# Taking the copied first chunk and the products of zeros out of the projections of a two-layer decoder trunk

## The chip, the core and the metric

The kernel runs on one core of a Trainium2 chip. The core has five engines that run side by side, each with its own list of instructions: TensorE (matmuls), VectorE, ScalarE, GpSimd and SyncE, which here issues nearly all DMAs. They wait for each other through semaphores. The metric is the device time of one execution in microseconds; less is better. Inputs lie in the chip's memory at the start, and the output must lie there at the end.

## What is computed

A trunk of two layers over one sequence of 256 tokens with 1024 features. Each layer has three sub-layers: a SwiGLU feed-forward block, a token mixer, and a second feed-forward block. The mixer of layer 0 is stick-breaking attention with 16 heads, that of layer 1 a Griffin block (a short convolution and a gated linear recurrence, RG-LRU) of width 1280. Each sub-layer normalizes its input, scales and shifts it by values worked out from a conditioning vector, and adds its gated result to the trunk. All is float32. Cut to what matters here:

```python
def swiglu(h, w_gu, w_down):
    g, u = jnp.split(h @ w_gu, 2, axis=-1)      # 1024 -> 2 x 2816
    return (jax.nn.silu(g) * u) @ w_down        # 2816 -> 1024
...
for layer in range(DEPTH):
    mod = (c_act @ mod_w[layer] + mod_b[layer]).reshape(B, N_SUB, 3, D_MODEL)
    h, g = sublayer_input(x, norm_g[layer, 0], mod[:, 0])
    x = x + MACARON_W * g * swiglu(h, ffn_w_gu[layer, 0], ffn_w_down[layer, 0])
    h, g = sublayer_input(x, norm_g[layer, 1], mod[:, 1])
    ...
    x = x + g * y                               # y: attention or RG-LRU block
    h, g = sublayer_input(x, norm_g[layer, 2], mod[:, 2])
    x = x + MACARON_W * g * swiglu(h, ffn_w_gu[layer, 1], ffn_w_down[layer, 1])
return rmsnorm(x, final_norm_g)
```

## The kernel before

**Products in three passes.** The products must be as exact as float32, and TensorE is used in a rounded form of it (float32r). So each operand is split in a rounded part and the rest: a weight into `wh` and `wl` (`load`, line 504; ScalarE writes `wh` at line 519, VectorE `wl` at line 522), an activation into a high and a low part. `group` (line 536, the matmul at line 548) then issues three matmuls that add up in one PSUM bank: `wh` with the high part, `wh` with the low part, `wl` with the high part. In the profile they show as two `wh` products and one `wl`, and I call them a group of three. Weights are the stationary operand (128x128), activations the moving one (128 features x 256 tokens).

**Layout.** Activations lie transposed: a chunk `hx` holds 128 of the 1024 features for all 256 tokens, so a normalized input has eight chunks, each with a high and a low tile. They come from a ring of 20 places, 320 words apart, with a pad ahead of it (`HXPAD`). The rings `wh` and `wl` have 7 places of 1024 words each. The results of an up tile go into the arena of the phase (`arenar`), which lies behind a pad of `ARPAD` words (line 487).

**Up tiles.** `up` (line 722) makes one tile of 256 results: over eight chunks `k` and two halves `g`, 8 x 2 x 3 = 48 matmuls. A feed-forward block has 22 such tiles, `f` = 0 to 21. Block 0 (layer 0, first feed-forward block) does tiles 0 to 7 together, chunk by chunk as the weights arrive, and from f=8 on goes tile by tile. The three other blocks (1 to 3 in the text), the attention and the RG-LRU block begin with `up_first` (line 737): two tiles from the input before normalization, 258 columns wide, whose results are scaled afterwards; the normalized chunks are made beside them, and from f=2 on `up` uses them.

**Down projections.** `down` (line 666) multiplies the results of the up tiles, two at a time, by the weights back to 1024 features: a block's is 22 x 8 x 3 = 528 matmuls in groups of three, the attention's and the RG-LRU block's are shorter. The last two weight tiles are taken feature by feature, so that residuals and the next input can begin (`residual`, line 689).

**The copied chunk and the products of zeros.** `other_copy` (line 660) copies the high and the low tile of chunk 0 of each normalized input to a ring of its own, `hk`, that lies behind `hx` and a pad of `HKPAD` words, one copy on ScalarE and one on VectorE (line 664). The up tiles whose `f` is in `KICKS` (line 37: 2, 3, 7, 9, 11, 15, 19), the attention's up tiles from the third on and the up tiles of the RG-LRU block take chunk 0 from `hk`, the others from `hx`; the values are the same. `kick_op` (line 731, the matmul at line 734) issues a product of zeros, 64 columns wide and bfloat16, that adds nothing to the bank; `down` puts one after its first group of three of a given weight tile: the first one in the feed-forward blocks, the second in the attention and in the RG-LRU block. So there are six copies of a chunk, 39 tiles that use one, and six products of zeros.

**Order.** The program first builds a list of operations with costs; `schedule` (line 167) is a list scheduler that gives each engine its order and each buffer its place; then the instructions are issued. TensorE's order keeps mostly to that of the program. DMAs go out on SyncE's queue in the order of the schedule, and each waits until its buffer is free; the loads for the conditioning (`rawm`, multiplied and summed on VectorE at line 580) lie between the weights' loads in that queue.

## Time and profile before

| | |
|---|---|
| median of 3 runs | 967.43 us (967.09 to 967.57) |
| the profiled execution | 973.06 us, its span 971.4 us |
| TensorE, matmuls | 8102, busy 98% of the span |
| of them 128x256 or 128x258 at line 548 | 3236 + 1618 on hx, 1664 + 832 on arenar, 234 on hk |
| VectorE, ScalarE | busy 82% and 58% |
| DMA | 251.25 MB, mean 259 GB/s over the span |
| feed-forward blocks, from first plain up tile to the end of down | block 0 about 61 to 202 us, block 1 about 333 to 501, block 2 about 518 to 685, block 3 about 792 to 960 |

A row of the groups view has the line, the engine and its operation, the output and inputs by name, the sizes and the number of instructions; after the bar the busy time in us and the mean length of one in ns; then the idle time of the engine just before them. A row of the timeline has the start in us, the length in us, and what ran; neighbours alike are merged, with their number. Matmuls overlap in it, since each lasts longer than the distance to the next: that distance, start to start, is the pitch. A row of the windows has the stretch, its length, the busy time of TensorE's matmuls and of its weight loads with the number of those that touch the stretch, the granted clock of TensorE as a share of full speed, the DMA engines' busy share and the rate in GB/s. A row of the chain in order of time has the start, the length and what the end of the kernel hung on then. A row of the waits has who waited for whom, the total in us, how often, and the longest.

### The profile page before, as it was taken

To read this page: it belongs to the slowest core of one execution; us is meant where nothing else is said; L and a number is where in the kernel's file an instruction comes from. 1 tells how busy PE (TensorE), PEld (TensorE's weight loads), DVE (VectorE), ACT (ScalarE), POOL (GpSimd) and SP (SyncE) were. 2 spreads that over 40 slices of the span, in tenths; PEclk is the share of its full clock that TensorE was granted. 3 is DMA by queue.
4 is the path that set the end of the run, shared out by engine and by line. 5 is a ranking of instruction groups with operands and counts; after the bars stand their busy time and mean duration, and the time that the engine had idled before them with its cause. 6 is when DMAs were issued, how large, how long until landed. Compare 5 with 4: busy or idle time off the path is not lost.

```text
span 971.4 us, 19751 instructions
## 1 busy us (share of the span) xinstructions
PE 951.9 (98%) x8102; PEld 938.5 (97%) x8102; DVE 797.0 (82%) x1325; ACT 562.7 (58%) x907; POOL 3.8 (0%) x16
## 2 busy tenths in 40 slices
PE   7999999999999999999999999999999999999996
PEld 5999999999999999999999999999999999999996
DVE  7899898798998999899789999844997997555443
ACT  4385444478987864454357544443879785444343
POOL 0000000000000000000000000000000000000000
PEclk9999999999999999999999999999999999999998
DMA  8999999864665489999967999955244646545421
GB/s 315 311 354 338 352 358 355 328 243 146 249 235 202 171 312 356 356 369 348 353 245 273 330 364 354 358 196 195 110 142 163 260 151 243 207 181 207 172 100 45
DMA packets 48189, 251.25 MB, mean 259 GB/s; under 512 B 5473, under 2 KB 6369, under 8 KB 28386
## 3 DMA queue, kind: packets, MB, share of 16 engines
q1 hardware_dynamic: 47378, 249.30, 69.7%
q8 instruction: 63, 1.03, 0.4%
q10 hardware_dynamic: 720, 0.69, 0.2%
q14 instruction: 28, 0.23, 0.1%
HBM read 248.92 MB, written 1.05 MB: 257 GB/s over the span
## 4 chain that ended last, share of the span: by engine, by line
PE 79%; DVE 8%; DMA 8%; ACT 3%; issue 2%; SPq 0%; DVEq 0%; ACTq 0%
PE bank L548 73%; DMA rawm<-in_modw 4%; DMA raw<-in_gu 3%; DVE wl L522 3%; PE bank L880 2%; DVE arenaf L1059 1%; DVE rawm L580 1%; PE bank L1003 1%; ACT arenaf L498 1%; ACT wh L519 1%; PE bank L565 1%; PE bank L956 1%; PE bank L981 1%; DMA x<-in_xT 1%; DVE hpre L650 0%
## 5 line engine op out<-in xcount | busy, mean ns | idle before, releaser
L548 PE MATMUL bank<-hx,wh 128*128 128x256 f32 (+1 forms) x3236 | 566.8, 279 | 5.0 <-ACT hx L498 3.4
L519 ACT ACTIVATE wh<-raw 128x1024 fp32r<-128x1024 f32 (+1 forms) x328 | 336.9, 1046 | 309.0 <-PE bank L548 208.9
L548 PEld LDWEIGHTS bank<-hx,wh 128*128 128x128 f32 x3236 | 494.7, 189 | 8.4 <-ACT hx L498 4.3
L522 DVE TENSOR_TENSOR wl<-raw,wh 128x1024 fp32r<-128x1024 f32 (+1 forms) x328 | 389.3, 1208 | 103.0 <-ACT wh L519 102.5
L548 PE MATMUL bank<-hx,wl 128*128 128x256 f32 (+1 forms) x1618 | 450.4, 278 | 0.0
L548 PEld LDWEIGHTS bank<-hx,wl 128*128 128x128 f32 x1618 | 306.6, 190 | 0.0
L548 PE MATMUL bank<-arenar,wh 128*128 128x256 f32 x1664 | 285.0, 277 | 0.0
L548 PEld LDWEIGHTS bank<-arenar,wh 128*128 128x128 f32 x1664 | 250.7, 188 | 0.1
L548 PE MATMUL bank<-arenar,wl 128*128 128x256 f32 x832 | 229.7, 276 | 0.0
L580 DVE SCALAR_TENSOR_TENSOR rawm<-rawm,cact 128x1024 f32<-128x1024 f32 x143 | 174.1, 1221 | 30.4 <-DMA rawm<-in_modw 29.7
L548 PEld LDWEIGHTS bank<-arenar,wl 128*128 128x128 f32 x832 | 156.2, 188 | 0.0
L498 ACT ACTIVATE arenar<-a 128x256 fp32r<-128x256 f32 x88 | 35.5, 405 | 8.6 <-DVE a L767 8.4
L772 DVE TENSOR_TENSOR arenar<-a,arenar 128x256 fp32r<-128x256 f32 x88 | 36.5, 419 | 0.6 <-ACT arenar L498 0.5
L767 DVE TENSOR_TENSOR a<-bank,sg 128x256 f32<-128x256 f32 x82 | 34.0, 418 | 0.5 <-ACT sg L498 0.4
L498 ACT ACTIVATE sg<-bank 128x256 f32<-128x256 f32 x82 | 29.7, 368 | 3.0 <-PE bank L548 3.0
L548 PE MATMUL bank<-hk,wh 128*128 128x256 f32 x156 | 31.2, 291 | 0.0
L498 ACT ACTIVATE hx<-x,mf 128x256 fp32r<-128x256 f32 x40 | 18.6, 500 | 20.2 <-DVE x L689 20.2
L498 ACT ACTIVATE hx<-hpre,mf 128x256 fp32r<-128x256 f32 x48 | 23.4, 500 | 10.5 <-DVE hpre L650 8.5
L689 DVE SCALAR_TENSOR_TENSOR x<-bank,mf,x 128x256 f32<-128x256 f32 x48 | 21.6, 478 | 7.8 <-PE bank L548 7.7
L548 PEld LDWEIGHTS bank<-hk,wh 128*128 128x128 f32 x156 | 24.0, 189 | 0.5
L652 DVE SCALAR_TENSOR_TENSOR hx<-hpre,mf,hx 128x256 fp32r<-128x256 f32 x48 | 22.9, 480 | 0.9 <-ACT hx L498 0.9
L880 PE MATMUL bank<-wh,hx 128*128 128x256 f32 x128 | 23.5, 281 | 0.0
(109 smaller groups left out, 541.0 us busy)
## 6 DMA issues: line engine op xcount, KB each, us to landing
raw<-in_gu SPq DMA_DIRECT2D x79, 1024.0 KB, 6.2
rawm<-in_modw SPq DMA_DIRECT2D x144, 512.0 KB, 6.8
raw<-in_wdn SPq DMA_DIRECT2D x44, 1024.0 KB, 6.6
raw<-in_win SPq DMA_DIRECT2D x10, 1024.0 KB, 4.8
raw<-in_qk SPq DMA_DIRECT2D x8, 1024.0 KB, 4.8
raw<-in_gu SPq DMA_DIRECT2D x14, 512.0 KB, 8.1
raw<-in_wout SPq DMA_DIRECT2D x5, 1024.0 KB, 5.1
raw<-in_wv SPq DMA_DIRECT2D x4, 1024.0 KB, 6.2
```

Source lines behind the costliest of these rows:

```text
L498: act.activation(o(), i(), f, **{k: (v() if callable(v) else v) for k, v in kw.items()})
L519: act.activation(h()[:, :m], raw()[:, a : a + m], AF.Copy)
L522: dve.tensor_tensor(lo()[:, :m], raw()[:, a : a + m], f32(h()[:, :m]), ALU.subtract)
L548: pe.matmul(o(b()), wc(u()), xc(v()), start=start and n == 0, stop=stop and n == len(passes) - 1, skip_group_check=True)
L565: pr.op("PE", c_mm(n, 4), lambda: pe.matmul(o(b()), wc(w()), xc(x32()), start=start, stop=stop, skip_group_check=True), [w, x32] + ([] if ...
L580: dve.scalar_tensor_tensor(raw(), raw(), 1.0, cact(), ALU.mult, ALU.mult, accum_out=m()[:, t : t + 1])
L652: V(lambda: dve.scalar_tensor_tensor(lo()[:, :T], hp(), sh()[:, c], f32(hi()[:, :T]), ALU.add, ALU.subtract), T, [hp, (sh, d), hi], [lo], ...
L689: dve.scalar_tensor_tensor(x[d](), acc.b()[:, j * T : (j + 1) * T], gate()[:, d : d + 1], x[d](), ALU.mult, ALU.add)
L767: V(lambda: dve.tensor_tensor(a(), b()[:, T:], sg(), ALU.mult), T, [(b, (1, 0)), sg], [a])
L772: V(lambda: dve.tensor_tensor(y[1](), a(), f32(y[0]()), ALU.subtract), n, [a, y[0]], [y[1]])
L880: pe.matmul(o, u()[:, tb * P : (tb + 1) * P], v()[:, c0 : c0 + 256], start=start and n == 0, stop=k == KD - 1 and n == 2, skip_group_check ...
L956: pe.matmul(zb[e]()[:, BL[i]], v()[rows, kc], w()[rows, qc], start=False, stop=i == 1 and n == 2, skip_group_check=True)
```

## The change

`other_copy`, `kick_op`, the ring `hk` with its pad, the list `KICKS` and the arguments that steered them go. All up tiles take chunk 0 from `hx`, and the down projections have no product of zeros. The ring and its pad took 528 words of each partition (16 and 2 x 256); `ARPAD` grows by 16, so that what comes after `pad1` moves by 512 words, and what lies between moves by 528.

```diff
-HXPAD, HKPAD, ARPAD = 112, 16, 184
-KICKS = (2, 3, 7, 9, 11, 15, 19)
+HXPAD, ARPAD = 112, 184 + 16
...
-    const.tile([P, HKPAD], F32, tag="pad2", name="pad2")
-    hkr, _ = ring("hk", 2, T, F32R)
...
         for d in range(KD):
             norm_chunk(gen, d, q)
-        other_copy(gen)
-
-    def other_copy(gen):
-        hi, lo = hcur[gen][0]
-        h2, l2 = hkick[gen] = Buf(hkr), Buf(hkr)
-        A(h2, lambda: f32(hi()[:, :T]), AF.Copy, T, [hi], [h2])
-        V(lambda: dve.tensor_copy(l2(), f32(lo()[:, :T])), T, [lo], [l2])
-
-    def down(l, s, nxt, srcs, ys, nlast, hook=None, post=None, n32=0, kicks=(0,)):
+
+    def down(l, s, nxt, srcs, ys, nlast, hook=None, post=None, n32=0):
...
                     for k in (2 * c, 2 * c + 1):
                         step(d, k)
-                        if d == 0 and k == 2 * c and c in kicks:
-                            kick_op(*place[d])
...
-    def up(acc, ws, gen, kick=False):
+    def up(acc, ws, gen):
...
-                h = hkick[gen] if kick and k == 0 and gen in hkick else hcur[gen][k]
...
-                      lambda u, c0=c0: u[:, c0 : c0 + P], h, lambda v: v[:, :T], T, k == KD - 1)
-
-    def kick_op(acc, j):
-
-        b = acc.b
-        pr.op("PE", 130.0, lambda: pe.matmul(b()[:, j * T : j * T + 64], zero, ident[:, :64], start=False, stop=False,
-                                             skip_group_check=True), [(b, "start")], [(b, j)])
+                      lambda u, c0=c0: u[:, c0 : c0 + P], hcur[gen][k], lambda v: v[:, :T], T, k == KD - 1)
...
-            other_copy((0, 0))
...
-            up(acc, load(gu[j, f], CH, f"gu_{j}_{f}", chained if j == 0 and f == f0 else None), (l, s), f in KICKS)
+            up(acc, load(gu[j, f], CH, f"gu_{j}_{f}", chained if j == 0 and f == f0 else None), (l, s))
```

The calls in `attention` and `rglru` lose the same argument.

More of the change, by code (lines that the diff above doesn't have):

```diff
@@ L601, in mod_final @@
             V(lambda: dve.tensor_scalar(fo(), mi(), 1.0, wt, ALU.add, ALU.mult), n, rr, ww)
-    ssq, hcur, gcur, hkick = {}, {}, {}, {}
+    ssq, hcur, gcur = {}, {}, {}
     def add_square(gen, d):
@@ L911, in q_proj @@
             acc = Acc(f"qk{f}")
-            up(acc, q_load(f), (l, s), True)
+            up(acc, q_load(f), (l, s))
             def put2(g, scale):
@@ L1038, in attention @@
         down(l, s, nxt, [wo[:, 2 * c : 2 * c + 2, :].rearrange("p k d -> p (k d)") for c in range(4)],
-             lambda k: (os_[k], slice(0, T)), 2, lambda c: hook(8 + c), tail, kicks=(1,))
+             lambda k: (os_[k], slice(0, T)), 2, lambda c: hook(8 + c), tail)
     def rglru(l, s, nxt):
@@ L1100, in xb_proj @@
                 acc = Acc(f"xb{n2}")
-                up(acc, load(win[1, n2], CH, f"xb{n2}"), (l, s), True)
+                up(acc, load(win[1, n2], CH, f"xb{n2}"), (l, s))
                 def evict(e, xb):
@@ L1110, in gate_proj @@
             acc = Acc(f"gt{n2}")
-            up(acc, load(win[0, n2], CH, f"gt{n2}"), (l, s), True)
+            up(acc, load(win[0, n2], CH, f"gt{n2}"), (l, s))
             b = acc.b
@@ L1168, in rglru @@
         down(l, s, nxt, [wout[:, 2 * c : 2 * c + 2, :].rearrange("p k d -> p (k d)") for c in range(NB)],
-             lambda k: ys[k], 2, n32=N32, kicks=(N32,))
+             lambda k: ys[k], 2, n32=N32)
     def final():
```

## The prediction

> **What bounds the kernel now.** I read the busy line of TensorE, the clock line and the chain of work that ended last on the page; then the chain in order of time; then, in short windows, the groups of matmuls by operands and the timeline of TensorE.
>
> ```profile
> PE 951.9 (98%) x8102; PEld 938.5 (97%) x8102; DVE 797.0 (82%) x1325; ACT 562.7 (58%) x907; POOL 3.8 (0%) x16
> ...
> PEclk9999999999999999999999999999999999999998
> ...
> PE 79%; DVE 8%; DMA 8%; ACT 3%; issue 2%; SPq 0%; DVEq 0%; ACTq 0%
> ```
>
> The chain is TensorE for 79% of the span. In order of time it is TensorE alone over whole feed-forward blocks (start, length, how many matmuls):
>
> ```profile
> 60.66 82.70 PE bank L548 x722
> 143.40 65.61 PE bank L548 x573
> ...
> 327.04 114.77 PE bank L548 x1008
> 443.64 7.98 DMA rawm<-in_modw
> ...
> 518.52 107.95 PE bank L548 x944
> 626.52 65.39 PE bank L548 x573
> ...
> 786.30 115.20 PE bank L548 x1011
> 901.55 56.90 PE bank L548 x501
> ```
>
> So the pitch of the matmuls (start to start) sets the time there, and nothing on the page tells the pitch. It isn't one number. These are the matmuls of 41 to 53 us, then those of 106 to 125 us, both 128x256 on the same tiles, and both windows' clock and counts:
>
> ```profile
> L548 PE MATMUL bank<-hx,wl 128*128 128x256 f32 x35 | 9.8, 281 | 0.0
> ...
> L548 PE MATMUL bank<-hx,wl 128*128 128x256 f32 x56 | 15.5, 276 | 0.0
> ...
> 41.00:53.00 12.00, 12.00 (x104) 12.00 (x104) 1.00 0.95 338
> 106.00:125.00 19.00, 19.00 (x170) 19.00 (x169) 1.00 0.92 339
> ```
>
> The granted clock is 1.00 in both, and neither idles, yet one lasts 281 ns and the other 276. The pitch itself comes from the first and last rows of the timeline of each stretch (the wl product of each group of three):
>
> ```profile
> 41.19 0.28 PE L548 MATMUL bank<-hx,wl 128*128 128x256 f32 x1
> ...
> 53.20 0.28 PE L548 MATMUL bank<-hx,wl 128*128 128x256 f32 x1
> ...
> 106.32 0.28 PE L548 MATMUL bank<-hx,wl 128*128 128x256 f32 x1
> ...
> 125.02 0.28 PE L548 MATMUL bank<-hx,wl 128*128 128x256 f32 x1
> ```
>
> Between the first pair lie 34 groups of three: 12.01 us / 102 = 117.7 ns. Between the second pair lie 55: 18.70 / 165 = 113.3 ns. I call them the slow and the fast pitch; the step is **4.4 ns a matmul**, 3.9%. Each holds for as long as nothing disturbs it, and the copied chunk is what moves the kernel from one to the other. The timeline where the first one runs:
>
> ```profile
> 71.48 0.28 PE L548 MATMUL bank<-hx,wl 128*128 128x256 f32 x1
> 71.60 0.40 PE L548 MATMUL bank<-hx,wh 128*128 128x256 f32 x2
> 71.83 0.28 PE L548 MATMUL bank<-hx,wl 128*128 128x256 f32 x1
> 71.95 0.40 PE L548 MATMUL bank<-hk,wh 128*128 128x256 f32 x2
> ...
> 73.26 0.28 PE L548 MATMUL bank<-hx,wl 128*128 128x256 f32 x1
> ...
> 73.60 0.28 PE L548 MATMUL bank<-hx,wl 128*128 128x256 f32 x1
> 73.94 0.28 PE L548 MATMUL bank<-hx,wl 128*128 128x256 f32 x1
> ```
>
> Ahead of hk a group takes 0.35 us, twelve matmuls after it began a group takes 0.34, and it stays so through f=10 to the next hk.
>
> **The change part by part.** *What it saves.* Two rows of ScalarE and VectorE go, six times each, and with them their wait; of these one VectorE copy (at 514.65) stands in the chain. An hk chunk met at the fast pitch costs a little, as the timeline of f=11 shows, and so does a product of zeros:
>
> ```profile
> PE bank L548 <- ACT hx L498: 3.4, 2, 2.6
> ...
> L664 DVE CAST hk<-hx 128x256 fp32r<-128x256 f32 x6 | 1.8, 292 | 0.1
> ...
> 104.58 0.28 PE L548 MATMUL bank<-hx,wl 128*128 128x256 f32 x1
> ...
> 105.98 0.28 PE L548 MATMUL bank<-hx,wl 128*128 128x256 f32 x1
> ...
> 143.08 0.28 PE L548 MATMUL bank<-arenar,wl 128*128 128x256 f32 x1
> 143.20 0.20 PE L734 MATMUL bank<-ident,zero 128*128 128x64 bf16 x1
> ...
> 143.91 0.28 PE L548 MATMUL bank<-arenar,wl 128*128 128x256 f32 x1
> ```
>
> From 104.58 to 105.98 are four groups: 1.40 us for 1.36, so 0.04 us; 21 of the 25 hk chunks in the feed-forward blocks meet the fast pitch (all but the first of each block): 0.85 us. From 143.08 to 143.91 are two groups and the zeros: 0.83 for 0.68, 0.15 us, six times 0.9 us. With the 0.29 us of the copy the change saves **2.0 us**. Nothing that is removed issued a DMA, no queue is moved past, and no wait is added. The buffers that follow move down by 2112 bytes, and the phase tiles by 2048; the chunks, the weights and the 256-wide products keep their place relative to each other, so I cost the move at 0, between nothing and the whole step of 4.4 ns if it counts. The planner gets fewer operations and may order some others differently; I cost that at 0 too, within 1 us either way (the longest wait of TensorE on ScalarE's hx is 2.6 us, in the first row of the fence).
>
> *What is late next.* What hk did has now to come about by itself. How the kernel enters a pitch when nothing is put in for it can be seen in three kinds of places: after a stall in the first block, in the attention's output projection, and in the wide tiles that open the other blocks. The windows are 29 to 33 us, 296.8 to 300.4 and 328 to 332:
>
> ```profile
> L548 PE MATMUL bank<-hx,wh 128*128 128x256 f32 x25 | 4.4, 276 | 0.0
> ...
> L548 PE MATMUL bank<-arenar,wl 128*128 128x256 f32 x10 | 2.8, 281 | 0.0
> ...
> L548 PE MATMUL bank<-hx,wl 128*128 128x258 f32 x12 | 3.4, 283 | 0.0
> ```
>
> And the timeline of the wide tiles, its first and last group in the last window:
>
> ```profile
> 328.20 0.28 PE L548 MATMUL bank<-hx,wl 128*128 128x258 f32 x1
> ...
> 332.16 0.28 PE L548 MATMUL bank<-hx,wl 128*128 128x258 f32 x1
> ```
>
> So the fast pitch does come unaided (29 us), the slow one also exists in a down projection (297 us: arenar, before its zeros), and the two wide tiles run at 283 ns, slower still. For f=9 of block 0 the forecast is plain: the timeline shows the slow pitch through all of f=8, over a tile's border, up to hk. For f=2 of blocks 1 to 3 the matmul before is a wide one at 283 ns, and which pitch follows is not shown. Bounds: 0 (fast at once) and 6.7 ns a matmul (the pitch of the wide tiles: 33 matmuls in 3.96 us from 328.20 to 332.16, 120.0 ns). I take 4.4, the only other pitch that plain 256-wide tiles show, and let it last into the down projection, since a border between tiles ends neither pitch.
>
> In the RG-LRU block the chain has another engine where the up tiles run:
>
> ```profile
> 708.28 1.59 DVE arenaf L1059 x4
> ...
> 736.46 6.72 ACT arenaf L498 x15
> ```
>
> *The sum.* An up tile has 8 chunks x 2 halves x 3 products = 48 matmuls, a down projection of a block 22 x 8 x 3 = 528.
> Block 0: 13 tiles (f=9 to 21) and down, 1152 x 4.4 ns = 5.1 us.
> Block 1: 20 tiles, 960 x 4.4 = 4.2 us; its down (2.3 us more) runs from 441 to 501 us, where the chain is the mod loads, not TensorE (443.64 above). TensorE then waits for those at the block's end (3.4 us on ScalarE's hx, above), so I count the down at 0; without that cover it costs its 2.3.
> Blocks 2 and 3: 1488 x 4.4 = 6.6 us each.
> Attention: six up tiles of 48 (each entered anew after other products, so half) and 192 in the output projection (half): 1.1 us.
> RG-LRU: its up tiles lie where the chain is VectorE's convolutions and ScalarE's exponentials, so 0; its output projection 192 x 4.4 = 0.8.
>
> Together 24.4 us, less 2.0: **+22.4 us**. The profiled execution took 973.06 us (span 971.4), 0.6% over the median of 967.43; on the median this gives 989.8, and I say **990 us**.
>
> *The skill against it.* The Trainium skill, page "TensorE: Matmul & The Clock Gate", section "Back-to-back issue gap", gives one gap for a width, N/2.4 + 2.5, which is 109 ns for 256 columns. Its page "SBUF — State Buffer", section "Who interferes with whom", has TensorE's two read ports independent and says that "PE and ACT never wait on anyone". By these the address of a chunk can't change a pitch, and the change would only save. The rows at 276 and 281 ns, one clock and one shape, speak against it.
>
> **The rivals.**
> *Faster: the fast pitch comes by itself.* If the first plain 256-wide matmuls after the wide tiles and after the stall near 60 us fall into the fast pitch, nothing is lost and the 2.0 us are saved: 965.4. For it: the row at 29 us, and that after hk's own uneven pitch (71.95 to 73.26) the plain chunks end in the fast one. Against it: all of f=8 at the slow pitch. It decides with the pitch of f=2 in blocks 1 to 3. The rule of the skill named above gives this result too. Chance 0.13.
> *Some blocks only.* Block 0 stays slow, which the trace nearly shows, and blocks 1 to 3 find the fast pitch (or one or two of them don't): 5.1 + 1.9 - 2.0 = +5.0, 972.4, and up to 984 with two of the other blocks at 6 each. Chance 0.28.
> *A still slower pitch.* The 120.0 ns of the wide tiles goes on into the plain ones of blocks 1 to 3: 2.2 ns more on 2880 up matmuls and two downs of 528, 8.7 us: 999. Against it: no plain tile of the trace shows 120. Chance 0.12.
> *The change doesn't do what it says*: it shifts addresses along with taking the copies away, so the pitch might move for that reason. It would show as a pitch that no tile of before has; it is within the cases above.
>
> **How the numbers follow.** Forecast 0.47, some blocks 0.28, faster 0.13, slower still 0.12. Leaving out the faster end and a part of the slowest, the range is 967 to 999. A measurement of this kernel can tell about 0.2% (1.9 us) from no change: the faster rival lies just at that edge, so I halve it, and give 0.03 of the mixed case to no change: faster 0.07, same 0.10, slower 0.83.
>
> **What would show it.** After the change: groups of hx matmuls at 281 ns and a triple of 0.35 us in windows in the middle of blocks 1, 2 and 3, and arenar at 281 in their downs, with the granted clock still 1.00; each TensorE piece of the chain longer by 3.9%; TensorE's waits no longer than before. I am wrong if blocks 1 to 3 show 276 with no hk in them, if the down projections return to 276 by themselves, or if what TensorE loses is found as waits of other engines.

## The result and the profile after

The changed kernel takes **971.75 us** (median of 10 executions, 969.84 to 980.76); the kernel before, beside it on the same chip, 967.5 (10 executions, 966.21 to 971.26). The ratio is 1.0053, 95% interval [1.0031, 1.0075]: slower, as forecast, but by 4 to 5 us and not by 22. In a second session both were run again: 968.74 (ratio 1.0003 [0.9987, 1.0019]) and 973.38 (1.0056 [1.0036, 1.0075]). Of all executions here one counts as slow, the profiled one of the kernel with copies in the mixers only (983.05 us, over 1.5% above that kernel's fastest, at the usual granted clock of 0.997), and the ratios leave it out.

The changed kernel's profiled execution took 971.68 us, its span is 970.0. Its page, the busy line, the clock and the chain's shares:

```profile
PE 949.2 (98%) x8096; PEld 935.1 (96%) x8096; DVE 794.7 (82%) x1319; ACT 561.3 (58%) x901; POOL 3.8 (0%) x16
...
PEclk9999999999999999999999999999999999999999
...
PE 72%; DMA 14%; DVE 10%; issue 3%; ACT 1%; SPq 0%; DVEq 0%; ACTq 0%
```

TensorE is busy 2.7 us less than before (951.9), and its share of the chain fell from 79% to 72%; DMA's rose from 8% to 14%. The chain in order of time, its long pieces:

```profile
61.27 51.75 PE bank L545 x454
119.59 8.25 DMA rawm<-in_modw
...
185.37 7.87 DMA rawm<-in_modw
...
327.63 98.30 PE bank L545 x864
427.86 8.44 DMA rawm<-in_modw
...
518.93 170.73 PE bank L545 x1499
...
785.31 171.75 PE bank L545 x1512
```

A long piece tells the pitch by itself: 98.30 us / 864 = 113.8 ns in block 1, 113.9 in block 2, 113.6 in block 3. Before, 114.77 / 1008 gave 113.9. There is no 3.9% in any of them. The matmul groups confirm it. The first two rows are 345 to 420 us (block 1's up tiles) and 445 to 495 (its down projection), the third is 758 to 777 us (the RG-LRU block's output projection); none of these stretches holds a copied chunk or a product of zeros:

```profile
L545 PE MATMUL bank<-hx,wl 128*128 128x256 f32 x221 | 61.0, 276 | 0.0
...
L545 PE MATMUL bank<-arenar,wl 128*128 128x256 f32 x148 | 40.8, 276 | 0.0
...
L545 PE MATMUL bank<-arenar,wl 128*128 128x256 f32 x54 | 15.2, 281 | 0.0
```

This is the sign that I had named for being wrong: 276 with no hk. All four feed-forward blocks of this execution run at the fast pitch from f=8 or f=3 to the end of the down projection. Only the RG-LRU block's output projection is slow, and half of the attention's up tiles (three of six).

So the time went elsewhere. Where the two traces part first is the stretch 40 to 80 us, at the end of the eight tiles that block 0 does together. The windows, with columns for TensorE's matmuls, its weight loads, VectorE, ScalarE, GpSimd, then the granted clock, DMA share and GB/s; first the kernel before, then the changed one:

```profile
40.00:62.00 22.00, 21.73 (x180) 21.12 (x179) 19.97 (x38) 12.74 (x17) 0.00 (x0) 1.00 0.96 346
62.00:80.00 18.00, 18.00 (x157) 18.00 (x157) 17.88 (x30) 14.80 (x28) 0.00 (x0) 1.00 0.87 334
```

```profile
40.00:62.00 22.00, 19.33 (x151) 18.06 (x152) 18.92 (x38) 11.34 (x14) 0.00 (x0) 1.00 0.93 315
62.00:80.00 18.00, 18.00 (x162) 18.00 (x161) 15.70 (x24) 14.27 (x28) 0.00 (x0) 1.00 0.82 303
```

In 40 to 62 us TensorE works 19.33 us instead of 21.73: 2.4 us of new idle time, at the same clock. These are waits for normalized chunks; in the kernel before the view of TensorE's waits is empty in this stretch:

```profile
PE bank L545 <- DVE hx L649: 1.8, 3, 0.9
PE bank L545 <- ACT hx L495: 0.7, 2, 0.4
```

The longest of them ends at 48.35 us. Here is what VectorE did just ahead of that chunk, before and then after, and the row of ScalarE, after, that it waited for:

```profile
46.22 1.22 DVE L522 TENSOR_TENSOR wl<-raw,wh 128x1024 fp32r<-128x1024 f32 x1
47.35 0.48 DVE L652 SCALAR_TENSOR_TENSOR hx<-hpre,mf,hx 128x256 fp32r<-128x256 f32 x1
```

```profile
46.67 1.23 DVE L519 TENSOR_TENSOR wl<-raw,wh 128x1024 fp32r<-128x1024 f32 x1 [1.07 <-ACT wh L516]
47.81 0.48 DVE L649 SCALAR_TENSOR_TENSOR hx<-hpre,mf,hx 128x256 fp32r<-128x256 f32 x1
...
45.58 1.06 ACT L516 ACTIVATE wh<-raw 128x1024 fp32r<-128x1024 f32 x1 [4.38 <-DMA raw<-in_gu]
```

In both a weight split stands ahead of the chunk. After, it waits 1.07 us for `wh`, since ScalarE waited 4.38 us for a weight to land (1.75 us at the same place before), and the chunk comes behind it.

From 62 to 80 TensorE is full in both, so nothing is lost there at once, but VectorE does 24 operations instead of 30 and the DMAs move 303 GB/s instead of 334. VectorE's timeline there, before and then after, shows the same pattern again:

```profile
63.46 0.42 DVE L767 TENSOR_TENSOR a<-bank,sg 128x256 f32<-128x256 f32 x1
63.80 1.22 DVE L522 TENSOR_TENSOR wl<-raw,wh 128x1024 fp32r<-128x1024 f32 x1
64.93 0.75 DVE L767 TENSOR_TENSOR a<-bank,sg 128x256 f32<-128x256 f32 x2
```

```profile
64.07 0.42 DVE L748 TENSOR_TENSOR a<-bank,sg 128x256 f32<-128x256 f32 x1
66.54 2.45 DVE L519 TENSOR_TENSOR wl<-raw,wh 128x1024 fp32r<-128x1024 f32 x2 [2.06 <-ACT wh L516]
68.90 0.42 DVE L748 TENSOR_TENSOR a<-bank,sg 128x256 f32<-128x256 f32 x1
```

Before, one weight split stands between the first and the second `a` product, and its `wh` is there. After, two splits stand there, and the first waits 2.06 us for ScalarE; the `a` products behind it wait too. ScalarE's timeline of the changed kernel has the same hole one step earlier, before a weight that has not landed:

```profile
62.83 0.38 ACT L495 ACTIVATE sg<-bank 128x256 f32<-128x256 f32 x1 [0.30 <-PE bank L545]
65.45 1.06 ACT L516 ACTIVATE wh<-raw 128x1024 fp32r<-128x1024 f32 x1 [2.23 <-DMA raw<-in_gu]
```

No operation was added there. The planner put the same operations in another order: numbered without the copies and the zeros, both kernels have the same 5080. Within block 0, 75 of VectorE's, 27 of ScalarE's and 28 of SyncE's loads lie in stretches whose order differs, and none of TensorE's; from the attention on it is 250, 164, 16, and 48 of TensorE's. On SyncE's queue the load of the parameters goes out with 14 weight loads ahead of it instead of 23, and the loads of the weights and of the conditioning change places in short stretches.

### The profile page after: what moved, and what is told of

The parts are those of the page before. It is cut to its first block, busy times and chain, and to the rows that moved or that the text cites. A ratio compares the mean times of both kernels' runs of the same rounds, so it can differ in the third digit from the quotient of the medians.

```text
span 970.0 us, 19708 instructions
## 1 busy us (share of the span) xinstructions
PE 949.2 (98%) x8096; PEld 935.1 (96%) x8096; DVE 794.7 (82%) x1319; ACT 561.3 (58%) x901; POOL 3.8 (0%) x16
## 4 chain that ended last, share of the span: by engine, by line
PE 72%; DMA 14%; DVE 10%; issue 3%; ACT 1%; SPq 0%; DVEq 0%; ACTq 0%
PE bank L545 65%; DMA rawm<-in_modw 10%; DMA raw<-in_gu 3%; DVE wl L519 3%; DVE rawm L577 2%; PE bank L860 2%; PE bank L1057 1%; PE bank L983 1%; PE bank L562 1%; DVE x L679 1%; PE bank L936 1%; DVE hx L649 1%; DVE hpre L647 1%; PE bank L961 1%; DVE hx L639 1%
## 5 line engine op out<-in xcount | busy, mean ns | idle before, releaser
L545 PE MATMUL bank<-hx,wh 128*128 128x256 f32 (+1 forms) x3392 | 592.4, 279 | 7.6 <-ACT hx L495 3.5
L545 PEld LDWEIGHTS bank<-hx,wh 128*128 128x128 f32 x3392 | 516.1, 189 | 12.8 <-DVE hx L649 5.7
L545 PE MATMUL bank<-hx,wl 128*128 128x256 f32 (+1 forms) x1696 | 470.8, 278 | 0.0
L545 PEld LDWEIGHTS bank<-hx,wl 128*128 128x128 f32 x1696 | 319.6, 188 | 0.0
L679 DVE SCALAR_TENSOR_TENSOR x<-bank,mf,x 128x256 f32<-128x256 f32 x48 | 21.6, 478 | 7.7 <-PE bank L545 7.6
L649 DVE SCALAR_TENSOR_TENSOR hx<-hpre,mf,hx 128x256 fp32r<-128x256 f32 x48 | 22.5, 477 | 1.4 <-ACT hx L495 1.4
L647 DVE SCALAR_TENSOR_TENSOR hpre<-x,mf,rst 128x256 f32<-128x256 f32 x48 | 21.9, 479 | 0.5
L495 ACT ACTIVATE arenaf<-arenaf 128x768 f32<-128x768 f32 (+1 forms) x31 | 22.0, 736 | 0.4
```

The source lines that it names most:

```text
L495: act.activation(o(), i(), f, **{k: (v() if callable(v) else v) for k, v in kw.items()})
L545: pe.matmul(o(b()), wc(u()), xc(v()), start=start and n == 0, stop=stop and n == len(passes) - 1, skip_group_check=True)
L647: V(lambda: dve.scalar_tensor_tensor(hp(), x[d](), gs()[:, c], q(), ALU.mult, ALU.mult), T, [x[d], (gs, d), q], [hp], ptr=1)
L649: V(lambda: dve.scalar_tensor_tensor(lo()[:, :T], hp(), sh()[:, c], f32(hi()[:, :T]), ALU.add, ALU.subtract), T, [hp, (sh, d), hi], [lo], ...
L679: dve.scalar_tensor_tensor(x[d](), acc.b()[:, j * T : (j + 1) * T], gate()[:, d : d + 1], x[d](), ALU.mult, ALU.add)
```

## The experiments

All ratios are to the kernel before, run beside each on the same chip. The kernels before and after, in the second session:

> The kernel before, run again with a profile of its own. Theory A (a pitch is entered anew at each stall or change of products and then held; hk makes each entry end in the fast one): about 967.5 us; blocks 0 to 3 at 276 ns from their first hk on, whatever pitch block 0 had before it. Rival B (what the change lost comes from the places that moved or from another order, not from the copies or zeros): also 967.5, so this run only gives the base and how much two profiles of one kernel differ ahead of 60 us.

> The changed kernel, run again with a profile of its own. Theory A: most runs 970 to 972 us, some 5 to 11 us longer, because block 0 (5.1 us) or block 2 (6.6 us), which begin behind a stall, enter the slow pitch by chance in some runs; if this profile is of a longer run, one of these blocks shows 281 ns through up tiles and down projection. Rival B: the longer runs show no block at 281, and the time is lost as waits.

The other ratios are to all runs of the kernel before in the same session, 17 to 33 each.

Two theories to begin with. **Pitch**: some stretches run slow without the copies, only fewer than forecast, and that is the 4 us. **Order**: the planner's other order costs them, whatever the pitch. In the recorded expectations the first is theory A; rival B is the order, at first together with the places; rival C puts the loss on the zeros, and rival D on late loads.

### Which part of the change costs: copies, zeros, places

The copies stay and the products of zeros go:

```diff
-                        if d == 0 and k == 2 * c and c in kicks:
+                        if d == 0 and k == 2 * c and c in ():
```

> The kernel before without its six products of zeros, the copied chunks kept. Theory A: the four blocks keep the fast pitch from up into down without them, so 4 x 0.15 us are saved; the RG-LRU block's output projection turns slow (0.8 us lost, as after the change) and the attention's has an uncertain 0.4: within 967 to 968.5, the same as before. Rival C (the zeros carry what the change lost): 970 to 972.

967.15 us, ratio 0.9990 [0.9974, 1.0006].

The zeros stay and the copies go, in the places of before:

```diff
-        other_copy(gen)
...
-                h = hkick[gen] if kick and k == 0 and gen in hkick else hcur[gen][k]
+                h = hcur[gen][k]
...
-            other_copy((0, 0))
```

> The kernel before with its zeros, but chunk 0 always from hx and no copies made; the two tiles stay allocated, so all places are those of before. Theory A: attention up tiles and the first RG-LRU tiles enter slow in part (1.3 us lost, less 0.85 saved), block 0 and block 2 by chance, with the down projections mended by the zeros: 968 to 970 us, single runs up to 3 or 4 us longer. Rival C (the zeros carry it all): 966.5 to 967. Rival B (places or order): as before, 967.5.

971.47 us, 1.0033 [1.0016, 1.0050]. The loss comes with the copies' removal and not with the zeros', though the time is 1.5 us above what theory A had expected at most. But this kernel also got the changed order, so the two theories stay.

The changed kernel in the places of before (the ring `hk` and its pad are kept and left empty):

```diff
-HXPAD, ARPAD = 112, 184 + 16
+HXPAD, HKPAD, ARPAD = 112, 16, 184
...
+    const.tile([P, HKPAD], F32, tag="pad2", name="pad2")
+    hkr, _ = ring("hk", 2, T, F32R)
```

> The changed kernel with the two tiles and their pad left allocated and unused, so that all places are those of before; order, copies and zeros as after the change. Theories A and B: as the changed kernel, 971 to 974 with single runs up to 980. Only if the moved places carry the loss: 967 to 968.5.

970.09 us, 1.0039 [1.0019, 1.0059]: beside the changed kernel's 1.0056 no difference that this can tell. The places that the change moved aren't the cause.

### How few copies do

All copies are made, but used only by f=8 in block 0 and f=3 in the others; the mixers as before, no zeros in the blocks:

```diff
-    def down(l, s, nxt, srcs, ys, nlast, hook=None, post=None, n32=0, kicks=(0,)):
+    def down(l, s, nxt, srcs, ys, nlast, hook=None, post=None, n32=0, kicks=()):
...
-            up(acc, load(gu[j, f], CH, f"gu_{j}_{f}", chained if j == 0 and f == f0 else None), (l, s), f in KICKS)
+            up(acc, load(gu[j, f], CH, f"gu_{j}_{f}", chained if j == 0 and f == f0 else None), (l, s), f == (8 if j == 0 else 3))
```

> The kernel before with far fewer disturbances: in the blocks one tile each takes the copied chunk (f=8 in block 0, f=3 in blocks 1 to 3) and no product of zeros; the attention and the RG-LRU block as before. Theory A (a pitch once entered is held, so one disturbance behind the last stall is enough): 21 copied chunks of 0.04 us and 4 products of 0.15 us less, so 1.2 us under before, and single runs spread no further than those of before. Rival D (the blocks up to block 2 run close to the DMA limit, so what TensorE saves there comes back as waits for late loads at the entry to the attention or to block 2): only block 3's part is left, 0.3 to 0.4 us.

**966.12 us, 0.9981 [0.9966, 0.9996]**: the lowest ratio here, though the intervals of the kernel without zeros and of the next one overlap it.

The same without any copies or zeros in the mixers:

```diff
-        other_copy(gen)
+        if gen not in ((0, 1), (1, 1)):
+            other_copy(gen)
...
-                        if d == 0 and k == 2 * c and c in kicks:
+                        if d == 0 and k == 2 * c and c in ():
...
-            up(acc, q_load(f), (l, s), True)
+            up(acc, q_load(f), (l, s))
...
-                up(acc, load(win[1, n2], CH, f"xb{n2}"), (l, s), True)
+                up(acc, load(win[1, n2], CH, f"xb{n2}"), (l, s))
...
-            up(acc, load(win[0, n2], CH, f"gt{n2}"), (l, s), True)
+            up(acc, load(win[0, n2], CH, f"gt{n2}"), (l, s))
```

> The changed kernel with the copied chunk put back in one tile of each block only (f=8 in block 0, f=3 in the others), none in the attention and the RG-LRU block, no zeros; places as before. Theory A (chance entries of blocks 0 and 2 make the longer runs of the changed kernel): the long runs are gone, all within 968.5 to 971.5, because the attention and the RG-LRU block still lose about 1.5 to 2 us. Rival D (late loads make the longer runs): 971 to 974 with single runs up to 977, as after the change.

967.35 us, 0.9985 [0.9972, 0.9998], below what both theories expected. Both kernels have the order of before in block 0. In it one use of the copy a block is enough, and the mixers need none; whether any copy is needed shows below.

The opposite: copies and zeros in the mixers only.

```diff
-        other_copy(gen)
+        if gen in ((0, 1), (1, 1)):
+            other_copy(gen)
...
-    def down(l, s, nxt, srcs, ys, nlast, hook=None, post=None, n32=0, kicks=(0,)):
+    def down(l, s, nxt, srcs, ys, nlast, hook=None, post=None, n32=0, kicks=()):
...
-            other_copy((0, 0))
...
-            up(acc, load(gu[j, f], CH, f"gu_{j}_{f}", chained if j == 0 and f == f0 else None), (l, s), f in KICKS)
+            up(acc, load(gu[j, f], CH, f"gu_{j}_{f}", chained if j == 0 and f == f0 else None), (l, s), False)
```

> The changed kernel with copied chunks and products of zeros put back in the attention and the RG-LRU block only; none in the blocks. Theory A: 1.5 to 2 us under the changed kernel, best runs at 967, but its long runs stay (block 0 or 2 entering slow: 5 and 6.6 us). Rival D: the same best runs, and long runs too, but with the blocks at 276 ns in a profile and the time in waits at the entries. If the longer runs go away here as well, both are wrong.

Eleven executions take 973.33 us (967.12 to 978.89), 1.0047 [1.0025, 1.0069], no less than the changed kernel, where 1.5 to 2 us less was expected. The profiled one took 983.05 us and shows what a block looks like that enters slow. Groups at 535 to 620 us and at 640 to 690:

```profile
L548 PE MATMUL bank<-hx,wl 128*128 128x256 f32 x242 | 68.0, 281 | 0.0
...
L548 PE MATMUL bank<-arenar,wl 128*128 128x256 f32 x143 | 40.2, 281 | 0.0
```

In the timeline block 2 has 117.78 ns from 526.7 to 696.1 us, 1438 matmuls without a break, up tiles and down projection: 6.4 us. So the slow block of the prediction exists, at about the price given there (6.6). How often it comes is counted below; three other kernels' profiles, of 973.76 to 977.03 us, show one as well.

### The pitch set by the place of the chunk

The changed kernel with the pad ahead of `hx` taken out and put behind (e5), so that the chunks, and the small buffers behind them up to the arenas, lie 448 bytes lower; weights and arenas stay:

```diff
-HXPAD, ARPAD = 112, 184 + 16
+HXPAD, ARPAD = 112, 184 + 16 + 112
...
-    const.tile([P, HXPAD], F32, tag="pad0", name="pad0")
```

> The changed kernel with the pad of 112 words ahead of the hx ring taken out and as many put into the pad ahead of the arenas, so that only the chunks move, by 448 bytes, to the kind of place the copied chunk had. Theory A with its cause in the place (the pitch depends on where the chunk lies against the weights): the plain up tiles of all blocks and mixers run at 119 to 120 ns, 3500 matmuls x 6 ns = about 21 us more, 990 to 996, the down projections fast again. If the place doesn't matter: 970 to 974.

1002.91 us, 1.0351 [1.0330, 1.0372]. Groups at 345 to 450 us (block 1's up tiles) and 460 to 500 (its down):

```profile
L544 PE MATMUL bank<-hx,wl 128*128 128x256 f32 x292 | 82.7, 283 | 0.0
...
L544 PE MATMUL bank<-arenar,wl 128*128 128x256 f32 x114 | 32.0, 281 | 0.0
```

The plain up tiles run at 120.00 ns (961 matmuls from 338.53 to 453.86 us), the wide tiles' pitch, which no plain tile of before had shown; the downs of blocks 1 to 3 at 117.78 behind them. The operations are the changed kernel's; the move alone costs 31 us, more than the 21 expected, because the down projections behind turned slow too (74 up tiles at 6.7 ns a matmul are 23.7 us, three downs at 4.4 ns 7.0). Of the buffers that moved, the chunks are the ones these tiles read; whether the others matter too wasn't tried apart. The formula that the prediction took from the Trainium skill, page "TensorE: Matmul & The Clock Gate", section "Back-to-back issue gap", goes by the width alone, and the page calls it that of an isolated matmul. The run shows that at one width and a granted clock of 0.997 the pitch in a stream depends on the place as well.

### Order against pitch

The kernel before with its whole plan (x), in which the copies and the zeros are planned and not issued. Some tiles read other values than the reference's, since the planner gives the place of chunk 0 away before they read it there:

```diff
-        h2, l2 = hkick[gen] = Buf(hkr), Buf(hkr)
-        A(h2, lambda: f32(hi()[:, :T]), AF.Copy, T, [hi], [h2])
-        V(lambda: dve.tensor_copy(l2(), f32(lo()[:, :T])), T, [lo], [l2])
+        h2, l2 = hkick[gen] = Same(hkr, hi), Same(hkr, lo)
+        pr.op("ACT", c_act(T), lambda: None, [hi], [h2])
+        V(lambda: None, T, [lo], [l2])
...
-        pr.op("PE", 130.0, lambda: pe.matmul(b()[:, j * T : j * T + 64], zero, ident[:, :64], start=False, stop=False,
-                                             skip_group_check=True), [(b, "start")], [(b, j)])
+        pr.op("PE", 130.0, lambda: None, [(b, "start")], [(b, j)])
```

> The schedule of the kernel before with nothing in the places of the copies and zeros: the planner still counts them, so all queues keep the order of before, but no copy and no product of zeros is issued and chunk 0 is read from hx. Theory A (the chance entries of blocks 0 and 2 into the slow pitch carry the loss): 971 to 974 us, single runs up to 980, as the changed kernel. Rival B (the planner, without the copies, put the mod loads later in the DMA queue of block 0, and that carries the loss): 967 to 969, since the RG-LRU block's 1.4 us are lost and about 1.5 saved; long runs only where an entry is slow.

967.90 us, 0.9994 [0.9979, 1.0009].

The changed kernel's plan with all copies and zeros issued (z), hung on to the operations ahead of them so that the planner doesn't see them:

```diff
+        if d == 0 and copied(gen):
+            also(a_op, lambda: act.activation(hkt[0], f32(hi()[:, :T]), AF.Copy))
+            also(v_op, lambda: dve.tensor_copy(hkt[1], f32(lo()[:, :T])))
...
+                            also(pr.last_pe, lambda b=place[0][0].b: pe.matmul(
+                                b()[:, :64], zero, ident[:, :64], start=False, stop=False, skip_group_check=True))
```

> The schedule of the changed kernel with all copies, copied chunks and products of zeros of the kernel before issued again inside neighbouring operations, so that the DMA queue keeps the order of the changed kernel. Theory A: 967 to 968.5 us, as before, no long runs. Rival B: 970 to 973, the loss stays though every block shows 276 ns after its first copied chunk; the time is lost up to the first plain tile, at the entry of the attention and of block 2.

973.00 us, 1.0048 [1.0033, 1.0064].

And the changed plan with copies in the blocks only, used at f=8 and f=3, without zeros; beside the last kernel:

```diff
     def copied(gen):
-        return True
+        return gen not in ((0, 1), (1, 1))
```

> The changed kernel's schedule with the copied chunk in one tile of each block only (f=8 in block 0, f=3 in the others). Theory A: 967 to 968, like the run with these same tiles in the order of before, and no long runs. Rival B: 970 to 972, because the order is that of the changed kernel, but the long runs (975 and more) are gone, since no block stays slow.

971.66 us (967.86 to 977.85), 1.0038 [1.0018, 1.0057]. I had expected the long executions to go with the copies; they stayed, and the profiled one (975.21 us) has all blocks fast and its loss in waits at the entries of the attention and of block 2.

With the kernels before and after, the first two settle the first question: **without any copy in the order of before nothing is lost; with all copies in the changed order all is lost.** On the way z shows what a copy does. Its block 2 ran slow from 520.6 us on. Groups at 522 to 543 us and at 550 to 600, and between them TensorE's timeline where the copied chunk (hk) of f=7 runs:

```profile
L548 PE MATMUL bank<-hx,wl 128*128 128x256 f32 x60 | 16.9, 281 | 0.0
...
L548 PE MATMUL bank<-hx,wl 128*128 128x256 f32 x141 | 39.0, 276 | 0.0
...
543.18 0.28 PE L548 MATMUL bank<-hx,wl 128*128 128x256 f32 x1
543.30 0.40 PE L738 MATMUL bank<-hk,wh 128*128 128x256 f32 x2
...
544.26 0.28 PE L548 MATMUL bank<-hx,wl 128*128 128x256 f32 x1
...
544.60 0.28 PE L548 MATMUL bank<-hx,wl 128*128 128x256 f32 x1
544.94 0.28 PE L548 MATMUL bank<-hx,wl 128*128 128x256 f32 x1
```

A group takes 0.35 us up to 543.18 and 0.34 from 544.26 on. The copied chunk of f=3, whose second group ran at 521.04 us, had not ended the slow pitch.

### Which part of the order

Four kernels move only loads on SyncE's queue and leave the other engines' orders. The kernel before with the parameters' load early, with the other shifts of the changed kernel, and with both; then the changed kernel with the shifts taken back. `resequenced` sorts the loads by a list of their kinds (weights, conditioning, parameters) and keeps all other queues:

```diff
-    order = pr.schedule()
+    order = resequenced(pr.schedule(), WANT)
```

> The kernel before, with all its copies and products of zeros, in which one load alone moves on SyncE's queue: that of the parameters (pars<-in_par) goes out with 14 weight loads of block 0 ahead of it, as in the changed kernel, and not with 23; the orders of the other engines stay. If this load ahead of the weights is what costs the 4 us: 971 to 973 us and a DMA rate of some 300 GB/s from 62 to 80 us of the span. If it is the shifts between weight loads and modulation loads, or the orders of ScalarE and VectorE: 967.5 to 969 us.

> The kernel before, with all its copies and products of zeros; on SyncE's queue the modulation loads and weight loads follow each other as in the changed kernel (some ten shifts by one place in blocks 0 to 2), and the load of the parameters keeps its place behind 23 weight loads. If the shifts are the cause: 971 to 973 us. If the parameters' load or the other engines' orders are: 967.5 to 969 us.

> The kernel before, with all its copies and products of zeros, and the whole order of SyncE's queue from the changed kernel; the orders of TensorE, VectorE, ScalarE and GpSimd stay as before. If the order of the loads is all of the loss: 971.5 to 974 us, as with the changed kernel's whole schedule and all copies (973.0). If the orders of ScalarE and VectorE carry it: 967.5 to 969 us.

> The changed kernel, without copies and zeros, in which the modulation and weight loads of SyncE's queue follow each other as before the change; the parameters' load stays early and the orders of TensorE, VectorE and ScalarE stay those of the changed kernel. If the shifts of modulation loads are the cause: 966 to 968.5 us. If the parameters' early load or the other engines' orders are: 970 to 972.5 us.

Called v1 to v4 here, in this order, they take 968.04 (0.9996 [0.9981, 1.0011]), **978.69** (1.0106 [1.0079, 1.0134]), **979.88** (1.0116 [1.0095, 1.0138]) and 973.65 (1.0053 [1.0032, 1.0073]). The parameters' load alone costs nothing. v2 and v3 came out far above what was expected of either cause: they lose 11.3 and 12.5 us, in another place. TensorE's waits of v3:

```profile
PE bank L1052 <- ACT arenar L547: 6.8, 1, 6.8
PE bank L597 <- ACT hx L547: 4.1, 2, 2.6
```

The 6.8 us are one wait in the attention, and v2 has it too (6.7 us). The attention lasts 127.5 and 128.4 us in them against 117.2. That these loads come in an order that the engines beside them aren't planned for is the likely reason; it wasn't tried apart. In the start, on the other hand, v3 runs as before, and v4, with the loads' shifts taken back, as changed; 40 to 62 and 62 to 80 us of v3, then of v4:

```profile
40.00:62.00 22.00, 22.00 (x188) 22.00 (x188) 20.91 (x42) 12.96 (x17) 0.00 (x0) 1.00 0.98 349
62.00:80.00 18.00, 18.00 (x158) 18.00 (x157) 17.88 (x30) 14.52 (x28) 0.00 (x0) 1.00 0.86 324
```

```profile
40.00:62.00 22.00, 19.84 (x160) 18.84 (x161) 19.38 (x39) 11.95 (x16) 0.00 (x0) 1.00 0.92 326
62.00:80.00 18.00, 18.00 (x162) 18.00 (x161) 14.87 (x23) 13.71 (x26) 0.00 (x0) 1.00 0.80 281
```

So the start's loss goes with what ScalarE and VectorE have in their queues, and the place of a load can't be tried apart from them without new waits. The last two kernels therefore move all engines together, in one part of the program only. Both are the changed kernel, without copies and zeros; the first (s1) has the operations of block 0 in the order of before, the second (s2) those from the attention on. `rearranged` puts the listed operations of each queue into the other plan's order:

```diff
-    order = pr.schedule()
+    order = rearranged(pr.ops, pr.schedule(), pr.loads)
```

> The changed kernel, without copies and products of zeros, in which the operations of block 0 stand on VectorE, ScalarE and SyncE in the order of the kernel before (75, 27 and 28 of them at another place); from the attention on all is as changed. If the loss comes from all orders together and part of it in block 0's start (1.8 us in the medians of the stages), 969 to 970.5 us, and the stretch from 62 to 80 us moves 330 to 350 GB/s again. If all of the loss begins in the start: 966 to 968. If none of it does: 971 to 972.5.

> The changed kernel, without copies and products of zeros, in which block 0 stays as changed and from the attention on the operations of TensorE, VectorE, ScalarE and SyncE stand in the order of the kernel before (48, 250, 164 and 16 of them at another place). If the loss comes from all orders together: 967.5 to 969.5 us, with the attention's entry and block 2's back at 117.2 and 180.7 us and the start's rate from 62 to 80 us still near 300 GB/s. If all of the loss begins in the start: 971 to 972.5. If none of it does: 966 to 968.

967.67 us (12 executions) and 972.93 (6). The windows of the first, then of the second:

```profile
40.00:62.00 22.00, 21.32 (x178) 20.53 (x178) 21.05 (x39) 13.70 (x19) 0.00 (x0) 1.00 0.92 341
62.00:80.00 18.00, 18.00 (x156) 18.00 (x154) 17.88 (x30) 14.12 (x26) 0.00 (x0) 1.00 0.94 362
```

```profile
40.00:62.00 22.00, 19.34 (x154) 18.06 (x153) 18.95 (x38) 11.06 (x15) 0.00 (x0) 1.00 0.93 318
62.00:80.00 18.00, 18.00 (x155) 18.00 (x154) 15.05 (x24) 13.86 (x26) 0.00 (x0) 1.00 0.84 299
```

**With block 0 in the order of before the loss is gone from most executions, and with all the rest in the order of before it is there.** The ratios are 1.0018 [0.9992, 1.0044] and 1.0052 [1.0031, 1.0073]. They overlap, because four of the first kernel's executions are long (972.1 to 979.5) while the other eight lie between 965.2 and 968.4; the second's lowest is 968.5. So these two point to block 0's start and don't settle it. The first kernel's profile is one of the long ones (973.76 us). Groups at 100 to 130 and 160 to 190 us:

```profile
L622 PE MATMUL bank<-hx,wl 128*128 128x256 f32 x86 | 24.2, 281 | 0.0
...
L622 PE MATMUL bank<-arenar,wl 128*128 128x256 f32 x85 | 23.9, 281 | 0.0
```

Block 0 came in slow and stayed so from 53.97 to 206.02 us. From the start of f=8 to its end it takes 141.33 us instead of 136.00: 5.33 us, which taken off leaves 968.4. The second kernel's profile (975.75 us) has the same slow block, so 5.33 us of it are pitch as well; the other long executions of both have no profile.

### What all twenty profiles show together

*The start.* In ten profiles block 0 has the order of before, in ten the changed one. From 40 to 62 us TensorE is busy 21.09 to 22.00 us in the first ten (median 21.6) and 19.19 to 20.01 in the others (19.65): 1.95 us lost, with no overlap. TensorE's waits for normalized chunks in this stretch are 0 to 0.9 us in the first ten and 1.6 to 2.9 in the others. From 62 to 80 us the DMAs move 319 to 375 GB/s and 275 to 304.

*The pitch.* Nine profiles are of kernels that use no copy in the blocks and leave the chunks where they lie to each other (one has before's zeros, one the mixers' copies). Of their 36 blocks four are slow up to the end of the down projection: block 0 in s1 and s2, block 2 in e7 (copies in the mixers only) and v4, each 1245 to 1438 matmuls, 5.5 to 6.4 us. So four of the nine executions have one, and blocks 1 and 3 never. Ten profiles are of kernels that use a copy in the blocks, and of their 40 blocks none is slow to its end; but block 2 of z ran slow over the copied chunk at 521.04 us, up to that at 543.30. (The twentieth is that of the kernel with the moved chunks.)

Block 0 comes to its f=8 at the slow pitch in six of the ten profiles with the order of before and in one of the other ten. So the f=8 that the prediction saw is no rarity in that order. The changed order's waits in 40 to 62 us start the stream anew more often, which may be why; no run shows it.

The stages of six of them in us, each from the trace's first matmul of the stage to that of the next (block 0 from its f=8, block 3 to the last matmul):

| | time | start to f=8 | block 0 | attention | block 1 | block 2 | RG-LRU | block 3 |
|---|---|---|---|---|---|---|---|---|
| before, second session | 968.55 | 65.8 | 136.31 | 117.18 | 181.07 | 181.07 | 93.95 | 182.58 |
| no copies, order of before (x) | 967.33 | 64.2 | 136.00 | 118.94 | 180.64 | 180.64 | 93.95 | 182.15 |
| changed | 971.68 | 66.7 | 136.00 | 118.52 | 180.67 | 181.79 | 95.21 | 182.20 |
| changed, second session | 970.71 | 65.1 | 136.00 | 117.23 | 180.67 | 183.59 | 95.22 | 182.20 |
| block 0 as before (s1) | 973.76 | 65.0 | 141.33 | 117.03 | 180.67 | 182.10 | 95.02 | 182.18 |
| the rest as before (s2) | 975.75 | 67.2 | 141.33 | 116.84 | 180.67 | 183.52 | 94.00 | 182.18 |

Over all profiles the median of the start is 64.9 us for the ten with the order of before in block 0 and 66.6 for the other ten: 1.7 us. The two ranges overlap, 63.4 to 66.3 and 65.1 to 68.0.

## Why the prediction was right in direction and wrong in size

**Right: the two pitches, and that they last.** 117.78 and 113.33 ns came back in every trace at a granted clock near 1.00, and a slow entry could go through all borders into the down projection (1438 matmuls in e7).

**Right: the price of a slow block.** 5.1 us forecast for block 0, 5.33 measured (f=8, which I had left out, is slow too); 6.6 for block 2, 6.4 measured. The RG-LRU's output projection was to lose 0.8 and lost 0.83 (188 matmuls x 4.4 ns).

**Right: the saving.** For the blocks it was 0.85 us for the copied chunks and 0.15 for each zeros: 1.45. Measured, from the table: 0.31 + 0.40 + 0.43 + 0.38 = 1.5 (row 1 against row 3, block 2 against row 2).

**Wrong: that the blocks enter slow.** This is the step that failed, "For f=9 of block 0 the forecast is plain" and, for f=2 of blocks 1 to 3, "I take 4.4, the only other pitch that plain 256-wide tiles show". In the changed kernel's two profiles all eight blocks find the fast pitch unaided, and so do 32 of 36 in the nine profiles without copies in the blocks. What I took for evidence was one profile, in which f=8 of block 0 was slow, as it often is in the order of before but not in the changed one, and which shows blocks 1 to 3 only with a copy in their first tiles. The copy isn't needed for the fast pitch; it mostly ends the slow one where that occurs. 22.5 of the 24.4 us rested on that step. The row at 29 us, quoted for the faster rival, was the better guide.

**Wrong: the order.** "The planner gets fewer operations and may order some others differently; I cost that at 0 too, within 1 us either way". It costs more than that in block 0's start alone, 1.7 to 2.0 us, and it is what made the change slower: x, z and the kernels before and after together show it, and s1 and s2 agree. So the right direction was luck: it came from the term that stood at 0, not from the blocks' pitch. In the changed kernel's profile, against row 1: +1.0 to f=8, +1.3 in the attention, +0.7 in block 2, +1.3 in the RG-LRU block (0.8 of it pitch, as forecast), and -1.1 in the other blocks, together +3.2, which is the difference of the two spans (970.0 and 966.8). How the rest beyond the start divides isn't settled: the attention's and block 2's entries differ by up to 2 us between executions, and block 2 is no shorter in s2, which has the order of before there.

**The faster rival** had 965.4 and a chance of 0.13. Its mechanism, the fast pitch by itself, came true in 32 of 36 blocks; x, which has it without the changed order, took 967.9. The rule of the Trainium skill's page "TensorE: Matmul & The Clock Gate", section "Back-to-back issue gap", gave that time too, but not for a reason that holds: more than one pitch exists at one width, and e5, in which the chunks moved, took 120.00 ns where the changed kernel took 113.33. The prediction read the formula as that of a stream, which the page doesn't say.

**The rival "some blocks only"** named 972.4, close to the 971.75. Its mechanism wasn't the one: in the changed kernel's two profiles no block is slow. Its longer executions, 974.6 to 980.8 us in the first session, have no profile; some of them may have a slow block, as four of the nine above do, so how much of its loss over many executions is pitch stays open.

**Open.** What in the start's order does it: the late weight, the weight split that waits for it in VectorE's queue and the chunk behind it are what the trace shows, but no kernel moved these alone. What makes an entry slow or fast, and what in the place of a chunk sets the pitch, wasn't found.

## What to carry to other kernels

When a list scheduler plans the kernel, taking any operation out is also a change of order everywhere behind it, so compare each engine's order of the two kernels first, and separate the two by planning operations that aren't issued. Before a step is priced at "always", count how often the trace shows it, over several profiles: a thing that repairs a state that comes only at times looks like the cause of the good one. And count it in the changed kernel's order too, where it can be rarer. And move loads together with the operations that use them: here the loads' order of one plan among the operations of the other cost 11.3 and 12.5 us.

## What the runs showed of the hardware

The same 128x256 float32r matmul has three pitches at the full granted clock, 113.33, 117.78 and 120.00 ns. Which of the first two holds could change where the stream starts anew after a stall (in z twelve matmuls up to 516.85 us run at the fast one, and those behind the wait of 0.22 us at 517.34 at the slow one, with no copied chunk between), and the slow one lasted for up to 1438 matmuls, over changes of weights, banks and moving operand. A chunk read from another place ended it at 71.95 us of the kernel before and at 543.30 us of z, and did not at 521.04 us of z. The third came in every plain up tile of the blocks when the chunks lay 448 bytes lower; that kernel took 31 us more.
